# Dilated attention of the odd layer: probabilities turned 64 rows at a time inside the next unit's burst of scores, sums of values one unit later

## The chip, the cores and the metric

The kernel runs on one core of a Trainium2 chip. TensorE multiplies matrices: it loads a stationary operand (a weight load) and streams a moving operand past it into a bank of PSUM. VectorE and ScalarE do elementwise work and read those banks out, GpSimd does a few small things, and SyncE issues the DMAs. The metric is the device time of one execution in microseconds (us), the median of several runs. Before the change it is 744.56 us (three runs, 744.52 to 745.54).

## The reference, cut to what matters

The program computes a trunk of two layers over 256 tokens of width 1024, in float32: an even layer (two kinds of attention), an MLP, the odd layer, an MLP, a last norm. The change lies in the odd layer's mixer:

```python
def odd_mixer(xn, w_in, w_o, cos_f, sin_f):
    hcat = (xn @ w_in).reshape(b, s, DIL_GROUPS, 3, DIL_HEADS, HEAD_DIM)   # 3 groups, q/k/v, 16 heads, 64
    q = apply_rope(hcat[:, :, :, 0], cos_f, sin_f)
    k = apply_rope(hcat[:, :, :, 1], cos_f, sin_f)
    v = hcat[:, :, :, 2]
    return dilated_attention(q, k, v) @ w_o
# dilated_attention, of each head and each of three windows (width 128 step 1, 512 step 4, 2048 step 16):
    sc = where(valid, einsum('bqhd,bqjhd->bhqj', q, k_sel) * scale, -1e30)
    m = max(sc); e = exp(sc - m); z = sum(e); o = einsum('bhqj,bqjhd->bqhd', e / z, v_sel)
    # the three o are added with the softmax of m + log z over the windows as weights
```

Mixing three softmaxes by their denominators is one softmax over all three windows' scores, and so the kernel computes it.

## The kernel before, in words

Tokens are put in an order in which the tokens of one step-4 or step-16 window lie in blocks of 64. A query tile of 128 tokens then has 256 scores for the first window (all tokens, masked) and 64 each for the other two (its own block of 64): 384 columns. Two heads make a **unit** `u`, and there are eight units. Each is worked through in these steps:

- `qk_steps` projects q and k: 12 steps of four pairs of matmuls (L186 of 512 columns, L187 of 256), each step half of a sum over 1024 into one bank `acc`; two steps make one (block, half) pair such as (0,0). `joined` (L193 on ScalarE, L194 on VectorE) reads the finished bank out into `qk`. After a block's second bank, `rope` swaps halves with four DMAs (`sw`, L848 and L849) and turns the result on VectorE (L850, L851, L853, L856); for block 0 it also splits `q0` into a high and a low part.
- `all_values` projects v: four steps of 12 matmuls of 384 columns (L180 to L182), two steps to a bank `acc`; L818 (VectorE) and four copies L821, L822 (ScalarE) read each bank out into `v0` and `v12`.
- `scores` makes the scores of both heads for both query tiles `i`: 12 matmuls for the first window (L201, contraction over 64 rows, so head `j` sits in its own half of TensorE's rows) and 16 calls of 64x64 for the other two (L880; each float32 call is two matmuls in the trace, 32 in all). Then come mask, negated minimum, exponential, sum and scaling (L887 to L891) into the probabilities `pp`, 128x384 for each `(i, j)`.
- `turn(i, j)` transposes the probabilities of one `(i, j)`: three 128x128 transposes on TensorE (L898, with `pp` as the stationary operand) into one bank `w`, then one copy into `pts` (L900, on whichever of ScalarE and VectorE the scheduler picks).
- `mix` sums values: eight calls of 64x128 and eight of 64x64 (L913, L918; in the trace 16 and 16) into one bank `acc`, then `split` writes the high part (ScalarE, L176) and the low part (VectorE, L177) into `mixed` (`oa` for units 0 to 3, `ob` for 4 to 7).

`weave` lays the attention of unit `u-1` between the 16 projection steps of unit `u`: after the first step the scores, with `mix(u-2)` as `other()` right behind their matmuls, and later four `turn` calls a few steps apart. The weights stream in throughout: SyncE loads a raw piece, ScalarE casts it to a high part `whi` (L176) and VectorE subtracts for the low part `wlo` (L177). ScalarE and VectorE take their instructions strictly in the order in which the scheduler put them, and so does TensorE.

PSUM has two rotating sets of four banks, tagged `w` and `acc`. A new tile takes the bank of the fourth tile of its tag before it, and the first matmul into it waits until that one has been read out. The last steps, `out_steps`, project the mixed heads (L180 to L182 with `oa` or `ob`), with the last unit's attention between them.

Of the kernel before, what the change touches and what calls it, by code (L numbers as in the profile page):

```python
# [16 lines left out]
F32 = mybir.dt.float32  # L17
F32R = mybir.dt.float32r
AF = mybir.ActivationFunctionType
ALU = mybir.AluOpType  # L20
# [3 lines left out]
P = 128  # L24
D = 1024
KT = D // P
T = 256
NT = T // P
HD = 64
# [15 lines left out]
def trunk(ctx, tc, a, out):  # L45
    nc = tc.nc
# [3 lines left out]
    work = ctx.enter_context(tc.tile_pool(name="work", bufs=2))  # L50
# [26 lines left out]
    def bank(tag):  # L77
        return ps.tile([P, 512], F32, tag=tag, name=tag)
# [17 lines left out]
    ident = const.tile([P, P], F32, name="ident")  # L96
# [99 lines left out]
    def two_heads(o, qk, ts):  # L196

        for n, (a, b) in enumerate(((0, 0), (0, 1), (1, 0))):
            for j in range(2):
                pb = slice(64 * j, 64 * j + 64)  # L200
                nc.tensor.matmul(o[j], qk[pb, 0, a, ts], qk[pb, 1, b, :], start=n == 0, stop=n == 2)  # L201
# [583 lines left out]
    def odd(op, xT, s):  # L785
# [3 lines left out]
        mask = op.tile([P, NT, 384], F32, name="mask")  # L789
# [36 lines left out]
        def qk_steps(d):  # L826


            hold = {}

            def gemm(b, f, half):
                if f == 0 and half == 0:
                    hold["w"], hold["s"] = weight(), scratch([2, T], "qk")
                if half == 0:
                    hold["p"] = bank("acc")
                (wh, wl), s, pq = hold["w"], hold["s"], hold["p"]
                for k in range(4 * half, 4 * half + 4):
                    ws = slice((f * KT + k) * P, (f * KT + k + 1) * P)
                    mm2(pq, wh[:, ws], wl[:, ws], xT[:, k], k == 0, k == KT - 1)
                if half == 1:  # L840
                    joined(s[:, f], pq)
                if f == 1 and half == 1:
                    rope(b, s)

            def rope(b, s):
                sw, r1 = scratch([2, T], "sw"), scratch([2, T], "r1")
                for r in range(0, P, 64):
                    nc.sync.dma_start(sw[r:r + 32], s[r + 32:r + 64])  # L848
                    nc.sync.dma_start(sw[r + 32:r + 64], s[r:r + 32])  # L849
                nc.vector.tensor_tensor(r1, s, cosT.unsqueeze(1).broadcast_to([P, 2, T]), op=ALU.mult)  # L850
                nc.vector.tensor_tensor(sw, sw, sinT.unsqueeze(1).broadcast_to([P, 2, T]), op=ALU.mult)  # L851
                if b == 0:
                    nc.vector.tensor_tensor(r1, r1, sw, op=ALU.add)  # L853
                    split(*halves(d["q0"]), r1)
                else:
                    nc.vector.tensor_tensor(d[("q12", "k12")[b - 1]], r1, sw, op=ALU.add)  # L856
# [7 lines left out]
        turned = {}  # L864

        def attention(u, d, other, pause=2):


            probs = {}

            def scores():
                ss = {(i, j): bank("w") for i in range(NT) for j in range(2)}
                for i in range(NT):
                    two_heads([ss[i, j][:, 0:T] for j in range(2)], d["q0"], tok(i))
                for i in range(NT):
                    for g in range(2):
                        for c in range(2):
                            for j in range(2):
                                pb, own = slice(64 * j, 64 * j + 64), slice(i * P + 64 * c, i * P + 64 * c + 64)
                                nc.tensor.matmul(ss[i, j][64 * c:64 * c + 64, T + 64 * g:T + 64 * g + 64], d["q12"][pb, g, own],  # L880
                                                 d["k12"][pb, g, own], start=True, stop=True)
                other()
                for i in range(NT):
                    for j in range(2):
                        sn, pp = scratch([384], "sn"), scratch([384], "pp")
                        mn, z, rz = (work.tile([P, 1], F32, tag=v, name=v, bufs=4) for v in ("dmn", "dz", "drz"))
                        nc.vector.tensor_tensor_reduce(out=sn, in0=ss[i, j][:, 0:384], in1=mask[:, i, :], op0=ALU.add, op1=ALU.min,  # L887
                                                       scale=-(HD ** -0.5), scalar=3e38, accum_out=mn)
                        nc.scalar.activation(pp, sn, AF.Exp, bias=mn, scale=-1.0, accum_out=z)
                        nc.vector.reciprocal(rz, z)  # L890
                        nc.scalar.activation(pp, pp, AF.Copy, scale=rz)  # L891
                        probs[i, j] = pp

            def turn(i, j):
                pp = probs.pop((i, j))
                pt = bank("w")
                for b in range(3):
                    nc.tensor.transpose(pt[:, b * P:(b + 1) * P], pp[:, b * P:(b + 1) * P], ident)  # L898
                pts = turned[u, i, j] = op.tile([P, 3, P], F32, tag="pts", name="pts", bufs=6)
                nc.any.tensor_copy(out=pts, in_=pt[:, 0:384].rearrange("p (b n) -> p b n", b=3))  # L900

            wait = lambda: None
            return [scores] + [wait] * pause + [f for i in range(NT) for j in range(2) for f in (lambda i=i, j=j: turn(i, j), wait)]

        def mix(u, d, out_tag):
            pvo = bank(out_tag)
            for i in range(NT):
                pts = [turned.pop((u, i, j)) for j in range(2)]
                at = i * P
                for kk in range(NT):  # L910
                    for j in range(2):
                        cs = slice(64 * j, 64 * j + 64)
                        nc.tensor.matmul(pvo[cs, tok(i)], d["v0"][:, kk, cs], pts[j][:, kk, :], start=kk == 0, stop=False)  # L913
                for c in range(2):
                    qs = slice(64 * c, 64 * c + 64)
                    for j in range(2):
                        cs = slice(64 * j, 64 * j + 64)
                        nc.tensor.matmul(pvo[cs, at + 64 * c:at + 64 * c + 64], d["v12"][:, 2 * i + c, cs], pts[j][:, 2, qs],  # L918
                                         start=False, stop=c == 1)
            split(*halves(mixed[u // 4][:, u % 4]), pvo[:, 0:T])  # L920

        d, nd = unit_tiles(0), unit_tiles(1)
        v0, v_out = value_steps(d)
        run_all(v0)
        r = [rstd(s)]
# [17 lines left out]
        return accs, out_last(accs, mixed, wo)  # L943

    def phase(name, fn, *args):
# [108 lines left out]
```

## Time and profile before

| | |
|---|---|
| median of 3 runs | 744.56 us |
| the profiled execution | 744.4 us |
| its span on the core | 742.6 us |
| TensorE matmuls busy | 734.6 us (99%) |
| VectorE busy | 536.2 us (72%) |
| ScalarE busy | 464.2 us (63%) |
| mean granted TensorE clock | 0.999 |

The odd layer's units lie between about 304 and 550 us of the span. In the timeline a row gives the start, the length from the first start to the last end, engine, line, operation, output and inputs, tile (rows by columns of TensorE), shape, and a count. Matmuls overlap, so the cost of a matmul is the distance from its start to the next one's, not its length. In a group's row the two numbers behind the bar are the busy time in us and the mean length of one in ns.

### The profile page before, as it was taken

The numbers are of one execution on the slowest core, as the hardware profiler recorded it, in microseconds if no ns is written. First come the engines' busy times: TensorE is split into PE (matmuls) and PEld (weight loads), VectorE is DVE, ScalarE is ACT, GpSimd is POOL, SyncE is SP. The second block draws the span as 40 slices with busy tenths as digits, with TensorE's granted clock in tenths as the row PEclk, the third lists the DMA queues.
The fourth block names the chain that finished last, engine by engine and source line by source line (L and its number), as shares of the span: only waits on it lengthen the run. The fifth ranks groups of instructions, "written<-read, shape, count | busy, mean of one in ns | idle before, by whom it ended". The sixth has DMA issues, their size and how long they took to land.

```text
span 742.6 us, 12516 instructions
## 1 busy us (share of the span) xinstructions
PE 734.6 (99%) x4764; PEld 645.2 (87%) x4764; DVE 536.2 (72%) x1108; ACT 464.2 (63%) x1044; POOL 6.0 (1%) x16
## 2 busy tenths in 40 slices
PE   9999999999999999999999999999999999999996
PEld 6998998888888888989899899898998888888885
DVE  6798869666665666898777787787769665665664
ACT  6679967554554556767775866877757544554541
POOL 0100000000000000000000000000000000000000
PEclk9999999999999999999999999999999999999999
DMA  8966334555555444674655555565653545455401
GB/s 286 344 205 222 114 121 163 186 212 180 178 209 185 179 174 150 197 249 154 224 185 183 188 189 179 171 189 192 232 199 126 215 169 209 169 190 193 178 26 56
DMA packets 28107, 136.87 MB, mean 184 GB/s; under 512 B 4496, under 2 KB 7056, under 8 KB 14992
## 3 DMA queue, kind: packets, MB, share of 16 engines
q1 hardware_dynamic: 27760, 135.81, 53.4%
q8 instruction: 37, 0.61, 0.3%
q10 hardware_dynamic: 288, 0.28, 0.1%
q14 instruction: 22, 0.18, 0.1%
HBM read 127.68 MB, written 1.05 MB: 173 GB/s over the span
## 4 chain that ended last, share of the span: by engine, by line
PE 91%; ACT 3%; DMA 2%; issue 1%; DVE 1%; SPq 0%; POOLq 0%; POOL 0%; DVEq 0%; ACTq 0%
PE w L186 16%; PE acc L180 13%; PE acc L181 13%; PE acc L182 13%; PE acc L186 12%; PE w L187 8%; PE acc L187 6%; PE w L898 1%; PE acc L913 1%; PE w L201 1%; DMA raw<-in_w_v 1%; PE w L730 1%; DMA bias<-in_rpb 1%; PE w L714 1%; ACT whi L176 1%
## 5 line engine op out<-in xcount | busy, mean ns | idle before, releaser
L177 DVE TENSOR_TENSOR wlo<-raw,whi 128x512 fp32r<-128x512 f32 (+3 forms) x488 | 302.5, 664 | 63.5 <-ACT whi L176 63.0
L176 ACT CAST whi<-raw 128x512 fp32r<-128x512 f32 (+3 forms) x488 | 263.7, 602 | 82.6 <-issue 71.1
L186 PE MATMUL w<-xT,whi 128*128 128x512 f32 x512 | 179.4, 394 | 0.0
L186 PE MATMUL acc<-xT,whi 128*128 128x512 f32 x384 | 137.3, 401 | 0.0
L187 PE MATMUL w<-xT,wlo 128*128 128x256 f32 x512 | 132.8, 280 | 0.0
L186 PEld LDWEIGHTS w<-xT,whi 128*128 128x128 f32 x512 | 93.6, 187 | 18.3
L187 PEld LDWEIGHTS w<-xT,wlo 128*128 128x128 f32 x512 | 96.1, 188 | 5.5
L187 PE MATMUL acc<-xT,wlo 128*128 128x256 f32 x384 | 99.8, 280 | 0.0
L180 PE MATMUL acc<-whi,h 128*128 128x512 f32 x250 | 98.4, 393 | 0.0
L181 PE MATMUL acc<-wlo,h 128*128 128x512 f32 x250 | 97.8, 391 | 0.0
L182 PE MATMUL acc<-whi,h 128*128 128x512 f32 x250 | 97.4, 390 | 0.0
L186 PEld LDWEIGHTS acc<-xT,whi 128*128 128x128 f32 x384 | 70.0, 188 | 12.7
L193 ACT COPY up<-w 128x256 f32<-128x256 f32 x64 | 23.9, 374 | 88.4 <-PE w L186 88.4
L187 PEld LDWEIGHTS acc<-xT,wlo 128*128 128x128 f32 x384 | 72.2, 188 | 3.7
L194 DVE TENSOR_TENSOR up<-up,w 128x256 f32<-128x256 f32 x64 | 26.8, 419 | 63.0 <-ACT up L193 62.3
L180 PE MATMUL acc<-whi,xT 128*128 128x384 f32 (+2 forms) x160 | 56.6, 354 | 0.1
L181 PE MATMUL acc<-wlo,xT 128*128 128x384 f32 (+2 forms) x160 | 56.1, 351 | 0.3 <-DVE wlo L177 0.2
L182 PEld LDWEIGHTS acc<-whi,h 128*128 128x128 f32 x250 | 46.9, 188 | 10.1
L181 PEld LDWEIGHTS acc<-wlo,h 128*128 128x128 f32 x250 | 47.0, 188 | 9.8
L182 PE MATMUL acc<-whi,xT 128*128 128x384 f32 (+2 forms) x160 | 55.4, 346 | 0.0
L180 PEld LDWEIGHTS acc<-whi,h 128*128 128x128 f32 x250 | 46.9, 188 | 9.1
L181 PEld LDWEIGHTS acc<-wlo,xT 128*128 128x128 f32 x160 | 30.3, 190 | 3.0 <-DVE wlo L177 2.0
(194 smaller groups left out, 1021.3 us busy)
## 6 DMA issues: line engine op xcount, KB each, us to landing
raw<-in_w SPq DMA_DIRECT2D x64, 1024.0 KB, 4.8
raw<-in_w_oqk SPq DMA_DIRECT2D x24, 1024.0 KB, 5.1
raw<-in_w_ov SPq DMA_DIRECT2D x16, 768.0 KB, 4.5
sw<-qk SPq DMA_DIRECT2D x96, 64.0 KB, 2.2
raw<-in_w_qk SPq DMA_DIRECT2D x4, 1024.0 KB, 10.8
raw<-in_w_oe SPq DMA_DIRECT2D x4, 1024.0 KB, 7.1
raw<-in_w_oo SPq DMA_DIRECT2D x4, 1024.0 KB, 5.0
bias<-in_rpb SPq DMA_DIRECT2D x8, 256.0 KB, 5.4
```

Source lines behind the costliest of these rows:

```text
L176: a = nc.scalar.copy(hi, src).ins
L177: return a, (eng or nc.vector).tensor_tensor(lo, src, hi.bitcast(F32), op=ALU.subtract).ins
L180: nc.tensor.matmul(o, sh, mh, start=first, stop=False)
L181: nc.tensor.matmul(o, sh, ml, start=False, stop=False)
L182: nc.tensor.matmul(o, sl, mh, start=False, stop=last)
L186: both = lambda: nc.tensor.matmul(o, sh, m.rearrange("p v n -> p (v n)"), start=first, stop=last)
L187: low = lambda: nc.tensor.matmul(o[:, 0:T], sl, m[:, 0, :], start=False, stop=False)
L193: nc.scalar.copy(dst, o[:, T:2 * T])
L194: nc.vector.tensor_tensor(dst, dst, o[:, 0:T], op=ALU.add)
L201: nc.tensor.matmul(o[j], qk[pb, 0, a, ts], qk[pb, 1, b, :], start=n == 0, stop=n == 2)
L714: nc.tensor.transpose(pt[:, b * P:(b + 1) * P], pp[:, b // 2, (b % 2) * P:(b % 2 + 1) * P], ident)
L730: nc.tensor.matmul(pvo[64 * j:64 * j + 64, o], v[:, kk, h * 64:(h + 1) * 64], pts[:, 2 * j + kk, :], start=kk == 0, stop=kk == NT - 1)
```

## The change

- `turn(u, i)` now turns both heads of a query tile: 12 transposes of 64 rows by 128 columns (L899 in the changed kernel), the two row halves `r` alternating, each half into a bank of its own, so that the two run in different halves of TensorE's rows. Two copies (L902) then put them into one `pts` of both heads. Each unit has 24 such transposes in place of 12, and four copies of 384 columns as before.
- The transposes of unit `u-1` go into the burst of scores of unit `u`: query tile 0 ahead of the L201 matmuls, query tile 1 between L201 and the 64x64 scores (now L877). They use `acc` banks, not `w`.
- `mix(u-2)` (now L912 and L917) moves from behind the scores to the start of the burst of unit `u`, so a unit's values are summed one unit later than before; `v0` and `v12` get three buffers each, `pp` gets four of its own, and `pts` two that each hold both heads.
- The burst of unit `u` stands behind the second projection step of the next unit (index 1), not the first; that of unit 7 stands inside unit 7's own values (index 13), and `mix(6)`, the turns of unit 7 and `mix(7)` among `out_steps`.

```diff
-                d[n] = op.tile(shape, dt, tag=n, name=n, bufs=2)
+                d[n] = op.tile(shape, dt, tag=n, name=n, bufs=3 if n[0] == "v" else 2)
...
-            def turn(i, j):
-                pp = probs.pop((i, j))
-                pt = bank("w")
+        def turn(u, i, tag):
+
+            pt = [bank(tag) for _ in range(2)]
+            for j in range(2):
+                pp = probs.pop((u, i, j))
                 for b in range(3):
-                    nc.tensor.transpose(pt[:, b * P:(b + 1) * P], pp[:, b * P:(b + 1) * P], ident)
-                pts = turned[u, i, j] = op.tile([P, 3, P], F32, tag="pts", name="pts", bufs=6)
-                nc.any.tensor_copy(out=pts, in_=pt[:, 0:384].rearrange("p (b n) -> p b n", b=3))
-
-            wait = lambda: None
-            return [scores] + [wait] * pause + [f for i in range(NT) for j in range(2) for f in (lambda i=i, j=j: turn(i, j), wait)]
+                    at = slice((3 * j + b) * 64, (3 * j + b) * 64 + 64)
+                    for r in range(2):
+                        rows = slice(64 * r, 64 * r + 64)
+                        nc.tensor.transpose(pt[r][:, at], pp[rows, b * P:(b + 1) * P], ident[rows, rows])
+            pts = turned[u, i] = op.tile([P, 6, P], F32, tag="pts", name="pts", bufs=2)
+            for r in range(2):
+                nc.any.tensor_copy(out=pts[:, :, 64 * r:64 * r + 64], in_=pt[r][:, 0:384].rearrange("p (b n) -> p b n", b=6))
...
-        weave(qk_steps(nd) + all_values(nd), attention(0, d, lambda: None, 3), 3)
-        for u in range(2, 8):
-            pd, d, nd = d, nd, unit_tiles(u)
-            side = attention(u - 1, d, lambda: mix(u - 2, pd, "acc"))
-
-            weave(qk_steps(nd) + all_values(nd), side + [lambda: mix(6, d, "acc")] if u == 7 else side)
+        def burst(u):
+
+            def step():
+                if u > 1:
+                    mix(u - 2, units[u - 2], "acc")
+                if u > 0:
+                    turn(u - 1, 0, "acc")
+                scores(u, units[u], lambda: turn(u - 1, 1, "acc") if u > 0 else None)
+            return step
+
+        for u in range(1, 8):
+            units.append(unit_tiles(u))
+            placed = {3 if u == 1 else 1: burst(u - 1)}
+            if u == 7:
+                placed[13] = burst(7)
+            beside(qk_steps(units[u]) + all_values(units[u]), placed)
         accs, wo = open_accs(), {}
-        side = attention(7, nd, lambda: None) + [lambda: mix(7, nd, "w")]
-        weave([f for k in range(6) for f in out_steps(accs, mixed, wo, k)], side)
+
+        def last_turn():
+            mix(6, units[6], "w")
+            for i in range(NT):
+                turn(7, i, "w")
+
+        beside([f for k in range(6) for f in out_steps(accs, mixed, wo, k)], {6: last_turn, 9: lambda: mix(7, units[7], "w")})
```

`beside(main, placed)` runs the main steps in order and a placed step behind the one of its index. In `scores(u, d, between)` the call `between()` stands between the two kinds of scores.

**TensorE, a burst in the middle of the layer.** A row gives a line, an operation, its output and inputs (numbered tensors are a unit's own) and the shape; `x12` counts repeats, and a bracket names the engine whose progress the first of them waits for. Before:

```order
L186 MATMUL acc<-xT,whi 128x512
L187 MATMUL acc<-xT,wlo 128x256
L201 MATMUL w<-q_4212 128x256 x6
L201 MATMUL w<-q_4212 128x256 [waits PE_49]
L201 MATMUL w<-q_4212 128x256 [waits Activation_49]
L201 MATMUL w<-q_4212 128x256 x4
L880 MATMUL w<-k_4214,q_4213 64x64 [waits DVE_49]
L880 MATMUL w<-k_4214,q_4213 64x64 x15
L913 MATMUL acc<-pts,v_3833 64x128 x4
L918 MATMUL acc<-pts,v_3834 64x64 x4
L913 MATMUL acc<-pts,v_3833 64x128 x4
L918 MATMUL acc<-pts,v_3834 64x64 x4
```

Now, at the same place:

```order
L912 MATMUL acc<-pts,v_3809 64x128 [waits PE_49]
L912 MATMUL acc<-pts,v_3809 64x128 x3
L917 MATMUL acc<-pts,v_3810 64x64 x4
L912 MATMUL acc<-pts,v_3809 64x128 x4
L917 MATMUL acc<-pts,v_3810 64x64 x4
L899 MATMUL acc<-ident,pp 128x64 [waits DVE_49,Activation_49] x2
L899 MATMUL acc<-ident,pp 128x64 x10
L201 MATMUL w<-q_4571 128x256 x12
L899 MATMUL acc<-ident,pp 128x64 [waits DVE_49] x2
L899 MATMUL acc<-ident,pp 128x64 x10
L877 MATMUL w<-k_4573,q_4572 64x64 x16
L186 MATMUL acc<-xT,whi 128x512 [waits Activation_49]
```

The values now come first, then the first turn, the L201 scores, the second turn and the 64x64 scores. The two first transposes of the second turn, one to each of its banks, wait for VectorE.

**VectorE, at the same place.** `sn` is the masked score, `qk` the projection's sum, `oa` the mixed heads, `v` the values. Before:

```order
L818 TENSOR_SCALAR v_4215<-acc,rstd 128x128
L177 TENSOR_TENSOR wlo<-raw,whi 128x512 x5
L887 ISA sn,dmn<-w,mask 128x384
L887 ISA dmn 128x1
L887 ISA sn,dmn<-w,mask 128x384
L887 ISA dmn 128x1
L887 ISA sn,dmn<-w,mask 128x384
L887 ISA dmn 128x1
L890 RECIPROCAL drz<-dz 128x1 x2
L177 TENSOR_TENSOR oa<-acc,oa 128x256
```

Now:

```order
L818 TENSOR_SCALAR v_4574<-acc,rstd 128x128
L856 TENSOR_TENSOR k_4573<-r_4871,sw 128x512
L177 TENSOR_TENSOR wlo<-raw,whi 128x512 x3
L194 TENSOR_TENSOR qk<-qk,acc 128x256
L177 TENSOR_TENSOR wlo<-raw,whi 128x512 x2
L177 TENSOR_TENSOR oa<-acc,oa 128x256
L177 TENSOR_TENSOR wlo<-raw,whi 128x512
L902 COPY pts<-acc 128x6x64
L883 ISA sn,dmn<-w,mask 128x384
L883 ISA dmn 128x1
```

The sum of bank (0,0) (L194) and the low part of the mixed heads (`oa`) now stand ahead of the masked scores, with two pieces of weights between them.

**ScalarE, at the same place.** Before:

```order
L176 CAST whi<-raw 128x512 x6
L821 ACTIVATE v_4598<-acc,rstd 64x128
L822 ACTIVATE v_4598<-acc,rstd 64x128
L821 ACTIVATE v_4598<-acc,rstd 64x128
L822 ACTIVATE v_4598<-acc,rstd 64x128
L176 CAST whi<-raw 128x512 x2
L889 ACTIVATE pp,dz<-sn,dmn 128x384 x2
L176 CAST oa<-acc 128x256
```

Now:

```order
L176 CAST whi<-raw 128x512 x6
L821 ACTIVATE v_4575<-acc,rstd 64x128
L822 ACTIVATE v_4575<-acc,rstd 64x128
L821 ACTIVATE v_4575<-acc,rstd 64x128
L822 ACTIVATE v_4575<-acc,rstd 64x128
L176 CAST whi<-raw 128x512
L193 COPY qk<-acc 128x256
L176 CAST whi<-raw 128x512
L176 CAST oa<-acc 128x256
L902 COPY pts<-acc 128x6x64 x3
```

The copies of the second value bank, a cast, the copy of bank (0,0) and another cast stand ahead of the high part of the mixed heads.

More of the change, by code (lines that the diff above doesn't have):

```diff
@@ new lines, in turn @@
+        def turn(u, i, tag):
+            pt = [bank(tag) for _ in range(2)]
+            for j in range(2):
+                pp = probs.pop((u, i, j))
+                for b in range(3):
+                    at = slice((3 * j + b) * 64, (3 * j + b) * 64 + 64)
[5 more added lines that the diff above has]
+                nc.any.tensor_copy(out=pts[:, :, 64 * r:64 * r + 64], in_=pt[r][:, 0:384].rearrange("p (b n) -> p b n", b=6))
@@ L907, in mix @@
             for i in range(NT):
-                pts = [turned.pop((u, i, j)) for j in range(2)]
+                pts = turned.pop((u, i))
                 at = i * P
@@ L912, in mix @@
                         cs = slice(64 * j, 64 * j + 64)
-                        nc.tensor.matmul(pvo[cs, tok(i)], d["v0"][:, kk, cs], pts[j][:, kk, :], start=kk == 0, stop=False)
+                        nc.tensor.matmul(pvo[cs, tok(i)], d["v0"][:, kk, cs], pts[:, 3 * j + kk, :], start=kk == 0, stop=False)
                 for c in range(2):
@@ L917, in mix @@
                         cs = slice(64 * j, 64 * j + 64)
-                        nc.tensor.matmul(pvo[cs, at + 64 * c:at + 64 * c + 64], d["v12"][:, 2 * i + c, cs], pts[j][:, 2, qs],
+                        nc.tensor.matmul(pvo[cs, at + 64 * c:at + 64 * c + 64], d["v12"][:, 2 * i + c, cs], pts[:, 3 * j + 2, qs],
                                          start=False, stop=c == 1)
             split(*halves(mixed[u // 4][:, u % 4]), pvo[:, 0:T])
-        d, nd = unit_tiles(0), unit_tiles(1)
+        units = [unit_tiles(0)]
+        d = units[0]
         v0, v_out = value_steps(d)
```

52 lines of the change are left out of this document (27 added, 25 removed).

## The prediction

> **What bounds the kernel now.** I read the page first, then the waits of TensorE, then its timeline through one unit of the odd layer, and last the timelines of ScalarE and VectorE there.
>
> ```profile
> span 742.6 us, 12516 instructions
> PE 734.6 (99%) x4764; PEld 645.2 (87%) x4764; DVE 536.2 (72%) x1108; ACT 464.2 (63%) x1044; POOL 6.0 (1%) x16
> ...
> PE w L880 <- DVE k L856: 0.2, 1, 0.2
> ```
>
> TensorE (PE) is busy for 99% of the span, and past the program's start the longest wait for another engine in its list is 0.2 us. So time is saved by taking slots off TensorE, and any new wait of TensorE costs its full length. A whole burst of scores, and one turn:
>
> ```profile
> 408.92 0.28 PE L187 MATMUL acc<-xT,wlo 128*128 128x256 f32 x1
> 409.13 0.98 PE L201 MATMUL w<-q 64*128 64x256 f32 x12
> 410.04 0.69 PE L880 MATMUL w<-k,q 64*64 64x64 f32 x32
> 410.67 0.66 PE L913 MATMUL acc<-pts,v 128*64 128x128 f32 x8
> ...
> 411.82 0.40 PE L918 MATMUL acc<-pts,v 128*64 128x64 f32 x8
> 412.15 0.50 PE L186 MATMUL acc<-xT,whi 128*128 128x512 f32 x1
> 412.49 0.28 PE L187 MATMUL acc<-xT,wlo 128*128 128x256 f32 x1
> ...
> 417.41 0.28 PE L187 MATMUL acc<-xT,wlo 128*128 128x256 f32 x1
> 417.53 0.39 PE L186 MATMUL acc<-xT,whi 128*128 128x512 f32 x1
> 417.76 0.28 PE L187 MATMUL acc<-xT,wlo 128*128 128x256 f32 x1
> 417.88 0.49 PE L898 MATMUL w<-ident,pp 128*128 128x128 f32 x3
> 418.13 0.48 PE L186 MATMUL acc<-xT,whi 128*128 128x512 f32 x1
> 418.44 0.28 PE L187 MATMUL acc<-xT,wlo 128*128 128x256 f32 x1
> ```
>
> Undisturbed, L187 to L187 takes 0.35 us (417.41 to 417.76): 0.12 for 256 columns and 0.23 for 512. The burst stretches that distance to 3.57 (408.92 to 412.49), so it costs 3.22: 0.09 on entering (0.21 less the slot of 0.12), L201 0.91, L880 0.63, the values 1.48, and 0.11 on leaving (0.34 less 0.23). A turn stretches it to 0.68 and costs 0.33, or 0.11 for each transpose; four turns make 1.32. Attention thus costs a unit 4.54 us of TensorE.
>
> **What a 64-row transpose costs.** No such transpose is in the trace; these groups bound it:
>
> ```profile
> L898 PE MATMUL w<-ident,pp 128*128 128x128 f32 x96 | 15.7, 272 | 0.1
> L880 PE MATMUL w<-k,q 64*64 64x64 f32 x256 | 5.6, 224 | 0.2 <-DVE k L856 0.2
> L898 PEld LDWEIGHTS w<-ident,pp 128*128 128x128 f32 x96 | 12.0, 140 | 1.8 <-ACT pp L891 0.3
> L201 PEld LDWEIGHTS w<-q 64*128 64x128 f32 x96 | 6.2, 185 | 1.9 <-issue 1.8
> L880 PEld LDWEIGHTS w<-k,q 64*64 64x64 f32 x256 | 4.5, 134 | 1.5 <-DVE k L856 0.5
> ```
>
> Streaming 64 columns of float32 in place of 128 shortens a matmul by about 50 ns (272 to 224). The load of a transpose (140) is nearly as short as that of 64 columns (134) and not like L201's 128 (185). L880 shows how fast tiles follow one another in separate parts of the array: 32 matmuls in groups of four, 0.63 us for eight groups, at most 0.08 each with entry and drain. L201 shows two heads side by side in the two row halves: 12 matmuls in 0.91 us is six pairs, where twelve slots of 0.12 would be 1.44. So a pair of 64-row transposes, the work of one old transpose, costs 0.055 to 0.08 if its load stays short, and 0.11, as now, if it doesn't. I take 0.06.
>
> The Trainium skill speaks against this: "TensorE: Matmul & The Clock Gate", section "LDWEIGHTS (loading the stationary operand)", gives a load P/1.2 ns by its P columns, whatever the rows. By it, as an estimate, a pair would cost at least 107 ns and nothing would be gained. The trace agrees for L201's loads and not for L898's, which are 45 ns shorter at equal columns; no row shows a half-height transpose.
>
> **The new burst without waits**, by the order on TensorE: entering 0.09, values 1.48, first turn 0.47 (six pairs of 0.06, 0.06 for the first load and 0.05 for L201's), L201 0.72 (six slots of 0.12, its entry and drain now in the turns), second turn 0.44 (six pairs and a drain of 0.08), 64x64 scores 0.63, leaving 0.11. That is 3.94 against 4.54: 0.60 saved. Five bursts (units 2 to 6) look so: 3.0 us.
>
> The ends, in the same prices: before, the values of units 6 and 7 stand alone, and so do unit 7's scores. For the values:
>
> ```profile
> 524.49 0.34 PE L182 MATMUL acc<-whi,xT 128*128 128x384 f32 x1
> 524.75 0.66 PE L913 MATMUL acc<-pts,v 128*64 128x128 f32 x8
> ...
> 526.24 0.44 PE L180 MATMUL acc<-whi,xT 128*128 128x384 f32 x1
> 526.52 0.34 PE L181 MATMUL acc<-wlo,xT 128*128 128x384 f32 x1
> ```
>
> That is 2.03 less two slots of 0.17: 1.68. Unit 0's scores are the same on both sides. From there, before: six bursts 19.3, two lone values 3.4, unit 7's scores 1.7 (0.09 + 0.91 + 0.63 + 0.11), 32 turns 10.6: 35.0. After: unit 1 without values 2.5, five bursts 19.7, unit 7 with its 64x64 scores ten rows later 3.3 + 0.8, values 6 with both last turns 2.5, values 7 1.7: 30.5. **Without waits the change saves 4.5 us.**
>
> **The wait that it adds.** `turn` now takes `acc` banks, four in rotation. Counted in the order of the code: projection (0,0), values, first turn (two), second turn (two). So the second turn's banks are those of projection (0,0) and of the values, and both must have been read out by then. Behind the waiting transposes stand the 64x64 scores and all projections. By the sums above the second turn is due 2.76 us after the burst starts (0.09 + 1.48 + 0.47 + 0.72). The values' bank is free when VectorE has written the low part of `oa`, and VectorE gets there only after L194 of (0,0) and two pieces of weights, and L194 only after ScalarE has finished the copies of the second value bank (L822), a cast and L193. When does L822 end, counted from the start of projection (0,0)?
>
> ```profile
> 351.39 0.36 ACT L822 ACTIVATE v<-acc,rstd 64x128 f32<-64x128 f32 x1
> 379.86 0.36 ACT L822 ACTIVATE v<-acc,rstd 64x128 f32<-64x128 f32 x1
> 411.16 0.36 ACT L822 ACTIVATE v<-acc,rstd 64x128 f32<-64x128 f32 x1
> 440.71 0.36 ACT L822 ACTIVATE v<-acc,rstd 64x128 f32<-64x128 f32 x1
> 470.46 0.36 ACT L822 ACTIVATE v<-acc,rstd 64x128 f32<-64x128 f32 x1
> 499.55 0.36 ACT L822 ACTIVATE v<-acc,rstd 64x128 f32<-64x128 f32 x1
> ...
> 348.05 0.40 PE L186 MATMUL acc<-xT,whi 128*128 128x512 f32 x1
> 377.84 0.40 PE L186 MATMUL acc<-xT,whi 128*128 128x512 f32 x1
> 407.64 0.40 PE L186 MATMUL acc<-xT,whi 128*128 128x512 f32 x1
> ```
>
> Projection (0,0) starts every 29.79 us (348.05, 377.84, 407.64), and L822 ends 3.7, 2.4, 3.9, 3.6, 3.6 and 2.9 us behind it. What follows has these lengths:
>
> ```profile
> 406.78 3.23 ACT L176 CAST whi<-raw 128x512 fp32r<-128x512 f32 x6
> ...
> 409.72 1.89 DVE L177 TENSOR_TENSOR wlo<-raw,whi 128x512 fp32r<-128x512 f32 x3
> ...
> L193 ACT COPY qk<-acc 128x256 f32<-128x256 f32 x48 | 17.2, 370 | 23.7 <-PE acc L186 23.7
> L194 DVE TENSOR_TENSOR qk<-qk,acc 128x256 f32<-128x256 f32 x48 | 19.5, 416 | 8.3 <-ACT qk L193 8.0
> L177 DVE TENSOR_TENSOR oa<-acc,oa 128x256 fp32r<-128x256 f32 x4 | 1.7, 425 | 0.7 <-ACT oa L176 0.7
> ```
>
> A cast 0.54 (3.23/6), L193 0.37, L194 0.35 to where VectorE can go on, two pieces 1.2 (1.89/3 each), the low part 0.43: 2.9. The bank is free 2.9 us after L822's end. It is due 5.57 after the start of (0,0): 2.81 for its eight pairs of 0.35, and 2.76. The wait is L822's lag less 2.67: 1.0, 0, 1.2, 0.9, 0.9, 0.2 by the six units, mean 0.7. I take 0.9, since the lag should grow: the masked scores now start behind a longer burst, and the copies, swaps and pieces queued behind them slip with them. A lower bound is 0.2 (the quickest pass of ScalarE's queue, six casts and four copies behind the first value step), an upper one 1.4. Five bursts: 4.5 us. At the ends the same banks cost about 2.2: unit 1 (the second turn comes sooner, 1.28 after the start, and needs only (0,0)) about 0.8, unit 7 about 0.8, the last turn behind `mix(6)` about 0.6 (L176 0.37, L177 0.43 and the way to ScalarE, less 0.4 for the first turn).
>
> The Trainium skill's "TensorEngine Tiling (Array Packing)", "PSUM Bottleneck", warns of just this, that faster tiles leave the reading of PSUM as the bound.
>
> **The sum:** -4.5 + 4.5 + 2.2 = +2.2 us on the profiled 744.4, or 746.7 on the median of 744.56.
>
> **What costs nothing.** The copies into `pts` keep number and width; each is wanted a unit later. SP issues unit 1's first value load four `sw` DMAs later, and weights are loaded four tiles ahead. A unit's probabilities are wanted 29 us after their scores. If a masked score came so late that it held a `w` bank, the next burst would show it; it has a unit's time.
>
> **The rivals.** (1) The gain stands and the waits are short: the fast lag of 2.4 becomes the rule, since ScalarE no longer waits for turns between the projections. With 0.2 a burst and 1.2 at the ends: -4.5 + 1.0 + 1.2 = -2.3, 742.3; with no wait at all 740.1. Against it: five of six lags are 2.9 or more. (2) Waits of half the size, 0.5 a burst and 1.9 at the ends: -0.1, 744.4. (3) The half-height load is as long as L201's, and a pair costs 0.11: 96 pairs give back 0.05 each, 4.8, while a later second turn shortens each of eight waits by 0.3, 2.4: 2.2 + 2.4 = +4.6, 749.2. That the two halves don't overlap at all would be slower still; L201's pairs speak against it.
>
> **How the numbers follow.** Forecast 0.42 (745.2 to 748.2 by waits of 0.6 to 1.2), rival 1 0.25, rival 2 0.18, rival 3 0.15. The limit of what can be told from no change is 0.2%, 1.5 us: 743.1 and 746.05. Slower: 0.30 of the forecast's share and rival 3's 0.15, 0.45. Same: 0.12 of the forecast's and 0.15 of rival 2, 0.27. Faster: 0.28. The range runs from rival 1 with waits near nothing to rival 3: 741.6 to 749.4.
>
> **What would show it.** In the changed trace: 24 L899 in two groups per burst, about 0.4 us each from first to last start (right) or 0.65 (rival 3); TensorE idle before the second group, released by VectorE's `oa` L177, near 0.9 us in most bursts; the distance of the bursts about 30.1 us (29.79 - 0.60 + 0.9). I am wrong if the list of TensorE's waits has no such row, or if the second turn's wait ends on something else.

## The result and the profile after

| | before | after |
|---|---|---|
| median, 6 runs each, same chip | 744.79 us (744.52 to 745.54) | 749.42 us (748.67 to 750.07) |
| ratio | | 1.006, 95% interval 1.005 to 1.007 |
| the profiled execution, and its span | 744.4, 742.6 us | 750.07, 748.3 us |

The change makes the kernel 4.6 us slower. The forecast was +2.2 us (746.7). The measured median lies at the upper end of the stated range of 741.6 to 749.4, and above the 745.2 to 748.2 that the forecast itself was given.

The page after the change (busy us, share of the span, instructions of each engine):

```profile
span 748.3 us, 12683 instructions
PE 733.3 (98%) x4860; PEld 642.4 (86%) x4860; DVE 538.7 (72%) x1113; ACT 462.6 (62%) x1039; POOL 6.1 (1%) x16
```

TensorE's waits after the change (what waited, for which engine's tile and line; us in total, times, longest):

```profile
PE acc L899 <- DVE oa L177: 3.0, 4, 0.7
PE acc L899 <- ACT pts L902: 1.2, 1, 1.2
...
PE acc L899 <- DVE ob L177: 0.8, 1, 0.8
```

TensorE is busy 1.3 us less (734.6 before) in a span that is 5.7 us longer. Before, its list held nothing above 0.2 us behind the start; now the transposes L899 wait five times for the low part of the mixed heads (`oa` L177 four times, `ob` L177 once), and once for a copy into `pts`. Here is one burst on TensorE, from the last projection ahead of it to the first pair behind:

```profile
410.19 0.40 PE L186 MATMUL acc<-xT,whi 128*128 128x512 f32 x1
410.51 0.66 PE L912 MATMUL acc<-pts,v 128*64 128x128 f32 x8
...
412.00 0.59 PE L899 MATMUL acc<-ident,pp 64*128 64x64 f32 x12
412.40 0.96 PE L201 MATMUL w<-q 64*128 64x256 f32 x12
413.20 0.21 PE L899 MATMUL acc<-ident,pp 64*128 64x64 f32 x1
414.16 0.58 PE L899 MATMUL acc<-ident,pp 64*128 64x64 f32 x11 [0.74 <-DVE oa L177]
414.67 0.69 PE L877 MATMUL w<-k,q 64*64 64x64 f32 x32
...
415.64 0.28 PE L187 MATMUL acc<-xT,wlo 128*128 128x256 f32 x1
```

The first turn takes 0.40 us (412.00 to 412.40) for six pairs, so 0.07 a pair with the way in. The second is let in with one transpose at 413.20, and the next comes at 414.16: it takes 1.47 us in all. From L186 to L187 the burst stretches 5.45 us (410.19 to 415.64) where the two projection slots of 0.23 would take 0.46 or 0.47: it costs 4.98, of which about 1.0 is the wait.

The same stretch on ScalarE and on VectorE shows what the second turn waits for:

```profile
410.71 0.36 ACT L822 ACTIVATE v<-acc,rstd 64x128 f32<-64x128 f32 x1
411.10 0.62 ACT L176 CAST whi<-raw 128x512 fp32r<-128x512 f32 x1
411.74 0.37 ACT L193 COPY qk<-acc 128x256 f32<-128x256 f32 x1
412.01 0.62 ACT L176 CAST whi<-raw 128x512 fp32r<-128x512 f32 x1
412.53 0.38 ACT L176 CAST oa<-acc 128x256 fp32r<-128x256 f32 x1
...
412.48 1.28 DVE L177 TENSOR_TENSOR wlo<-raw,whi 128x512 fp32r<-128x512 f32 x2
413.69 0.42 DVE L177 TENSOR_TENSOR oa<-acc,oa 128x256 fp32r<-128x256 f32 x1
```

The low part ends at 414.11 (413.69 + 0.42) and the transposes go on at 414.16. Bursts 2 to 6 all look like this: their first L912 stand at 380.19, 410.51, 440.85, 471.18 and 501.51, 30.33 us apart, where the distance before was 29.79.

**Where the 4.6 us lie.** From the first L201 of the odd layer to the layer's last projection of mixed heads, TensorE took 231.4 us before and 235.9 after: 4.55 more. The profiled execution after the change had also lost 1.15 us ahead of that point, where nothing was changed. Over the nine profiled executions of this case that point lies between 325.0 and 326.7 us, so this is the spread of runs. In the layer, measured between the first value steps of the units, the start (to unit 1's first value step) gained 0.94, the next stretch 0.56, the five bursts lost 0.54 each (2.7), and the end from unit 7's values on lost 3.34.

### The profile page after: what moved, and what is told of

Read it like the earlier page. It is cut to its first block, busy times and chain, and to the rows that moved or that the text cites. A ratio compares the mean times of both kernels' runs of the same rounds, so it can differ in the third digit from the quotient of the medians.

```text
span 748.3 us, 12683 instructions
## 1 busy us (share of the span) xinstructions
PE 733.3 (98%) x4860; PEld 642.4 (86%) x4860; DVE 538.7 (72%) x1113; ACT 462.6 (62%) x1039; POOL 6.1 (1%) x16
## 4 chain that ended last, share of the span: by engine, by line
PE 86%; ACT 7%; DVE 3%; issue 1%; DMA 1%; SPq 0%; POOLq 0%; POOL 0%; DVEq 0%
PE w L186 16%; PE acc L180 13%; PE acc L181 13%; PE acc L182 13%; PE acc L186 10%; PE w L187 8%; PE acc L187 5%; ACT whi L176 3%; DMA raw<-in_w_c 1%; DVE wlo L177 1%; PE w L714 1%; PE w L730 1%; ACT v L822 1%; ACT v L821 1%; PE w L877 1%
## 5 line engine op out<-in xcount | busy, mean ns | idle before, releaser
L177 DVE TENSOR_TENSOR wlo<-raw,whi 128x512 fp32r<-128x512 f32 (+3 forms) x488 | 303.6, 665 | 72.7 <-ACT whi L176 71.7
L186 PE MATMUL w<-xT,whi 128*128 128x512 f32 x512 | 179.4, 394 | 0.0
L186 PE MATMUL acc<-xT,whi 128*128 128x512 f32 x384 | 134.6, 396 | 0.0
L187 PE MATMUL w<-xT,wlo 128*128 128x256 f32 x512 | 132.8, 280 | 0.0
L186 PEld LDWEIGHTS w<-xT,whi 128*128 128x128 f32 x512 | 93.6, 187 | 18.3
L187 PEld LDWEIGHTS w<-xT,wlo 128*128 128x128 f32 x512 | 96.1, 188 | 5.5
L187 PE MATMUL acc<-xT,wlo 128*128 128x256 f32 x384 | 99.8, 280 | 0.0
L181 PE MATMUL acc<-wlo,h 128*128 128x512 f32 x250 | 97.8, 391 | 0.0
L186 PEld LDWEIGHTS acc<-xT,whi 128*128 128x128 f32 x384 | 69.8, 187 | 13.6
L193 ACT COPY up<-w 128x256 f32<-128x256 f32 x64 | 23.9, 374 | 88.6 <-PE w L186 88.6
L187 PEld LDWEIGHTS acc<-xT,wlo 128*128 128x128 f32 x384 | 72.0, 188 | 3.8
L194 DVE TENSOR_TENSOR up<-up,w 128x256 f32<-128x256 f32 x64 | 26.9, 420 | 62.9 <-ACT up L193 62.0
L181 PE MATMUL acc<-wlo,xT 128*128 128x384 f32 (+2 forms) x160 | 56.1, 351 | 0.6 <-DVE wlo L177 0.6
L181 PEld LDWEIGHTS acc<-wlo,h 128*128 128x128 f32 x250 | 47.0, 188 | 9.8
L193 ACT COPY qk<-acc 128x256 f32<-128x256 f32 x48 | 17.7, 368 | 30.8 <-PE acc L186 30.6
```

Source lines behind the costliest of these rows:

```text
L177: return a, (eng or nc.vector).tensor_tensor(lo, src, hi.bitcast(F32), op=ALU.subtract).ins
L181: nc.tensor.matmul(o, sh, ml, start=False, stop=False)
L186: both = lambda: nc.tensor.matmul(o, sh, m.rearrange("p v n -> p (v n)"), start=first, stop=last)
L187: low = lambda: nc.tensor.matmul(o[:, 0:T], sl, m[:, 0, :], start=False, stop=False)
L193: nc.scalar.copy(dst, o[:, T:2 * T])
L194: nc.vector.tensor_tensor(dst, dst, o[:, 0:T], op=ALU.add)
```

## The experiments

Each is compared with the kernel before on the same chip; for the first four that is 744.88 us, for the last three 744.93. "After" below is the changed kernel.

### 1. Take away what makes the second turn wait

The weight pieces of the next tile are held back until the mixed heads' two parts and the copies into `pts` have been issued, on ScalarE and VectorE alike; the copies into `pts` get fixed engines (three on ScalarE, one on VectorE).

```diff
-        prefetch(j + LOAD_AHEAD, j + SPLIT_AHEAD)
+        behind = state.pop("behind", ())
+        with ExitStack() as held:
+            for ins in behind:
+                held.enter_context(tc.issue_after(ins))
+            prefetch(j + LOAD_AHEAD, j + SPLIT_AHEAD)
...
-                nc.any.tensor_copy(out=pts[:, :, 64 * r:64 * r + 64], ...)
+                copy = nc.vector.tensor_copy if i and r else nc.scalar.copy
+                done = copy(pts[:, :, 64 * r:64 * r + 64], ...).ins
+                state["behind"] = state.get("behind", ()) + (done,)
...
-                    mix(u - 2, units[u - 2], "acc")
+                    state["behind"] = mix(u - 2, units[u - 2], "acc")
```

> The changed kernel with one thing moved: the weight pieces that ScalarE and VectorE had ahead of the mixed heads' split are held behind that split and behind the copies of the turned probabilities (which get fixed engines, as the scheduler had them: three on ScalarE, one on VectorE). TensorE's order stays as it is. Theory (the second turn waits for the values' bank because two weight pieces and the late copy of projection (0,0) stand ahead of it): the wait of about 1.0 us per burst in the changed kernel falls to 0.2 or less, the distance of bursts from 30.33 to about 29.4 us, the time from 749.4 to 743.5 to 745. Rival (the wait belongs to the bank rotation, whatever stands in the queues, or it moves to the next projection's bank): the distance stays at 30 us or more, the time above 748.

Measured: 742.84 us (742.44 to 743.94), ratio 0.9971 (0.996 to 0.9983), a little below the 743.5 to 745 that the theory gave. The timeline of a burst on TensorE, and the low part on VectorE (lines are shifted by four: L903 is L899, L205 is L201, L881 is L877, L190 is L186, L181 is L177):

```profile
408.26 0.40 PE L190 MATMUL acc<-xT,whi 128*128 128x512 f32 x1
...
410.08 0.58 PE L903 MATMUL acc<-ident,pp 64*128 64x64 f32 x12
410.47 0.96 PE L205 MATMUL w<-q 64*128 64x256 f32 x12
411.28 0.53 PE L903 MATMUL acc<-ident,pp 64*128 64x64 f32 x12
411.74 0.69 PE L881 MATMUL w<-k,q 64*64 64x64 f32 x32
...
412.70 0.28 PE L191 MATMUL acc<-xT,wlo 128*128 128x256 f32 x1
...
410.60 0.42 DVE L181 TENSOR_TENSOR oa<-acc,oa 128x256 fp32r<-128x256 f32 x1 [1.07 <-ACT oa L180]
```

The low part ends at 411.02, ahead of the second turn, which now takes 0.46 us. The burst costs 3.97 (408.26 to 412.70, less 0.47); the prediction's price without waits was 3.94. The bursts stand 29.33 apart. So the changed kernel's loss of 4.6 us, and a gain of 2 us that it hid, hang on the order on two engines that are 62% and 72% busy.

### 2. The same order with whole-height transposes

```diff
-                    at = slice((3 * j + b) * 64, (3 * j + b) * 64 + 64)
-                    for r in range(2):
-                        rows = slice(64 * r, 64 * r + 64)
-                        nc.tensor.transpose(pt[r][:, at], pp[rows, b * P:(b + 1) * P], ident[rows, rows])
+                    nc.tensor.transpose(pt[j][:, b * P:(b + 1) * P], pp[:, b * P:(b + 1) * P], ident)
```

> The changed kernel with 128x128 transposes in place of those of 64 rows, one bank for each head; places, banks and order otherwise as in the change. Theory (a 64-row pair costs 0.06 us where a whole transpose costs 0.11, and the wait swallows what that saves): each turn 0.7 to 0.8 us long in place of 0.4, with two more changes of tile shape, but the second turn's wait falls from about 1.0 to 0.1 to 0.4, so that the distance of bursts stays within 0.3 us of 30.33 and the time at 749 to 751.5. Rival (the two row halves don't run side by side, so the halving saves nothing): turns as long as now, the time unchanged or lower by the waits, 745 to 748.

Measured: 748.91 us (748.77 to 749.31), ratio 1.005 (1.0034 to 1.0067), just below the 749 to 751.5 that were expected. The two turns of a burst (L896):

```profile
411.35 0.87 PE L896 MATMUL acc<-ident,pp 128*128 128x128 f32 x6
412.15 0.97 PE L201 MATMUL w<-q 64*128 64x256 f32 x12
413.05 0.88 PE L896 MATMUL acc<-ident,pp 128*128 128x128 f32 x6
413.85 0.69 PE L877 MATMUL w<-k,q 64*64 64x64 f32 x32
```

Each turn takes 0.80 us, L201 0.90 in place of 0.80, and the second turn comes late enough that it waits for nothing: the list of waits has no row for `oa`, only one of 0.5 us for a copy into `pts`. The bursts stand 30.17 apart. So the short transposes are worth 0.84 us a burst (the distance of 30.17 less 29.33 of experiment 1), which is just what the three pieces add up to: 0.80 + 0.90 + 0.80 against 0.40 + 0.80 + 0.46. The two kernels lie 6.1 us apart (748.91 less 742.84), but they also differ in the order of the weight pieces and in the waits outside these bursts, so 6.1 is not the price of the transposes alone. In the changed kernel the wait takes the whole gain back: 749.42 with half heights, 748.91 with whole ones.

### 3. Half heights alone

The kernel before with each transpose split into two of 64 rows into two `w` banks; where they stand and when values are summed stays as before.

```diff
-                pt = bank("w")
+                pt = [bank("w") for _ in range(2)]
...
-                    nc.tensor.transpose(pt[:, b * P:(b + 1) * P], pp[:, b * P:(b + 1) * P], ident)
+                    for r in range(2):
+                        rows = slice(64 * r, 64 * r + 64)
+                        nc.tensor.transpose(pt[r][:, b * 64:b * 64 + 64], pp[rows, b * P:(b + 1) * P], ident[rows, rows])
```

> The kernel before with the 64-row transposes alone: each of the 32 turns stays where it was, between projections, as six transposes of 64 rows into two w banks with a copy from each. Theory (a pair costs 0.06, but entering and leaving the half-height tile shape costs 0.09 + 0.06 and 0.08 + 0.11): a turn costs about 0.5 us in place of 0.33, 32 x 0.17 = 5.5 us more, 749 to 751. Rival (a change of tile shape costs nothing of its own): a turn costs 0.2, 740 to 741.

Measured: 751.30 us (751.11 to 751.47), ratio 1.0082 (1.0067 to 1.0097), 0.3 above the theory's range. One turn among the projections:

```profile
390.09 0.28 PE L187 MATMUL acc<-xT,wlo 128*128 128x256 f32 x1
390.30 0.40 PE L900 MATMUL w<-ident,pp 64*128 64x64 f32 x6
390.63 0.50 PE L186 MATMUL acc<-xT,whi 128*128 128x512 f32 x1
390.97 0.28 PE L187 MATMUL acc<-xT,wlo 128*128 128x256 f32 x1
```

L187 to L187 takes 0.88 us, so a turn costs 0.53 (less 0.35 for the pair), where the whole-height turn cost 0.33. Entering adds 0.09 (0.21 less the slot of 0.12), three pairs take 0.33, leaving adds 0.11. Thirty-two turns at 0.20 more make 6.4 us, and the kernel is 6.4 us slower. In the changed kernel's burst there are twelve in a row, and none of their neighbours is a tile of 128x128. Ahead of L201, whose tile shape (64 rows by 128) is theirs too, they take 0.40 us, behind it 0.46 (experiment 1), and between the values and the 64x64 scores, neither of their shape, 0.52 (experiment 4); six whole-height ones take 0.80 in the burst (experiment 2). So the move into the burst is not a detail of the change: where the turns stood before, the short transposes lose. No run has twelve in a row among projections, so how much of the loss is due to the short run and how much to the neighbours is not shown.

### 4. Leave the weights as they are and move the values away

Here `mix` stands between L201 and the second turn, so its bank is no longer the one that the second turn takes; `pts` gets a third buffer.

```diff
-                if u > 1:
-                    mix(u - 2, units[u - 2], "acc")
                 if u > 0:
                     turn(u - 1, 0, "acc")
-                scores(u, units[u], lambda: turn(u - 1, 1, "acc") if u > 0 else None)
+                scores(u, units[u], between)   # between: mix(u - 2, ...), then turn(u - 1, 1, "acc")
```

> The changed kernel with the values moved from the start of the burst to between the L201 scores and the second turn, so that the second turn's banks are those of projection (0,0) and of the first turn, and three pts buffers. Theory (which bank is due when decides the wait): the second turn comes 3.0 us after the start, its banks are free at about 2.1 and 2.8 us, so its wait falls to 0.2 or less; one more change of tile shape costs 0.1 to 0.2; the distance of bursts 29.4 to 29.6 and the time 744.5 to 746. Rival (VectorE is late by a fixed amount and any second turn waits for it): the wait stays near 1 us and the time at 749 or above.

Measured: 745.45 us (744.74 to 746.09, 10 runs), ratio 1.0005 (0.9995 to 1.0014). The burst has one more change of tile shape, and in four bursts of five no wait at the second turn:

```profile
411.52 0.59 PE L899 MATMUL acc<-ident,pp 64*128 64x64 f32 x12
412.04 0.69 PE L877 MATMUL w<-k,q 64*64 64x64 f32 x32
...
411.18 1.89 DVE L177 TENSOR_TENSOR wlo<-raw,whi 128x512 fp32r<-128x512 f32 x3
412.98 0.42 DVE L177 TENSOR_TENSOR oa<-acc,oa 128x256 fp32r<-128x256 f32 x1
```

The second turn takes 0.52 us and the bursts stand 29.47 apart. One is 29.88: there the second turn takes 0.93, since ScalarE's queue is 0.66 us later against projection (0,0) and the copy of the first turn, whose bank the second one takes, comes late with it. Of the 4.6 us lost, 4.0 come back, though nothing holds the weight pieces: three of them still stand ahead of the low part of the mixed heads, which ends at 413.40, almost 2 us behind the start of the second turn. TensorE doesn't wait for it, because the values' bank is no longer the one that is due. That the wait was for the values' bank is shown by this and the first experiment from two sides. Unit 1's wait of 1.2 us for a copy into `pts`, which this edit doesn't touch, stands in its list of waits as before.

### 5. Hold the weights back on VectorE alone

As experiment 1, but the pieces wait only for the low part of the mixed heads, on VectorE; ScalarE's order is that of the changed kernel.

```diff
-                    mix(u - 2, units[u - 2], "acc")
+                    state["behind"] = mix(u - 2, units[u - 2], "acc")[1:]   # the low part alone
```

> The changed kernel with the next tile's low weight pieces held only on VectorE, behind the low part of the mixed heads; ScalarE's order is as in the changed kernel. Theory (the wait is mostly VectorE's two pieces of 0.6 us that stand between L194 and the low part): the low part then ends about 1.2 us earlier, the second turn's wait falls from 1.0 to at most 0.3 us, the bursts stand 29.4 to 29.7 us apart, and the whole takes 743.5 to 746 us. Rival (ScalarE's late copies L822 and casts decide, and VectorE's pieces only fill the time until they arrive): the wait stays at 0.7 us or more, the bursts stay 30.0 us or more apart, 747.5 to 749.5 us.

Measured: 748.43 us (747.89 to 749.37), ratio 1.0049 (1.0034 to 1.0064): the rival's time, and not the theory's. The bursts are not alike, and neither forecast fits all of them: they stand 29.91, 30.88, 30.08, 29.60 and 29.58 apart. The second of them on the three engines (lines shifted by three):

```profile
406.34 0.40 PE L189 MATMUL acc<-xT,whi 128*128 128x512 f32 x1
...
413.46 0.59 PE L902 MATMUL acc<-ident,pp 64*128 64x64 f32 x11 [0.53 <-DVE oa L180]
...
406.39 3.22 ACT L179 CAST whi<-raw 128x512 fp32r<-128x512 f32 x6
...
412.57 0.38 ACT L179 CAST oa<-acc 128x256 fp32r<-128x256 f32 x1
...
412.98 0.42 DVE L180 TENSOR_TENSOR oa<-acc,oa 128x256 fp32r<-128x256 f32 x1 [0.37 <-ACT oa L179]
```

VectorE now runs the low part as soon as ScalarE's high part is there (412.95), so its two pieces no longer delay it. But ScalarE is late itself: its six casts begin at 406.39, with projection (0,0) of 406.34, and in the changed kernel they begin 1.2 us ahead of it (406.35 against 407.58, rows below). In this burst, the worst of the five, the first turn waits for ScalarE too: it takes 0.73 us in place of 0.40, held by the copies L825 of the second value bank. In the two last bursts, where ScalarE kept its old place, the low part ended 5.78 us after the start of (0,0) in place of 6.53, and the wait fell to about 0.3 us as expected (a second turn of 0.73 less 0.46); in the other three ScalarE's queue had slipped by 0.3 to 1.3 us and the second turn waited 0.6 to 0.85.

```profile
407.58 0.40 PE L186 MATMUL acc<-xT,whi 128*128 128x512 f32 x1
...
406.35 3.23 ACT L176 CAST whi<-raw 128x512 fp32r<-128x512 f32 x6
```

So VectorE's two pieces are worth 0.75 us of the wait where nothing else moves. What is left there, about 0.3, went in experiment 1, where ScalarE's casts were held as well and no burst waited; no run held ScalarE alone. What made ScalarE slip in three bursts of this kernel isn't settled: its copies of the first value bank wait there for VectorE's L821, which is itself late by 1.3 us against TensorE, and no run followed that further back.

### 6. The ends

Experiment 1's kernel, with `mix(6)` two output steps earlier and the last turns and `mix(7)` one later; experiment 1's kernel ran beside it again.

```diff
-            mix(6, units[6], "w")
-        beside(..., {6: last_turn, 9: lambda: mix(7, units[7], "w")})
+        beside(..., {4: lambda: mix(6, units[6], "w"), 7: last_turn, 10: lambda: mix(7, units[7], "w")})
```

> The first experiment's kernel (weight pieces held on both engines), with unit 6's values two steps earlier among the output steps and both last turns and unit 7's values one step later, so that the reading of unit 6's values has about 3 steps of cover before the last turns need their banks. If the waits that are left at the end come from too little distance between values and turns: the last turns run in 0.9 to 1.0 us without a wait, one more change of tile shape costs about 0.2, and it takes 0.3 to 0.7 us less than the first experiment's kernel on the same chip, 742.2 to 742.6 us. If what is left at the end is a wait for ScalarE's late casts of weights and mixed heads, the wait moves to the next output step and the time is the same within 0.2 us.

> The first experiment's kernel once more, beside the other two on the same chip: 742.4 to 743.2 us.

Measured: 742.42 us (741.89 to 743.12), ratio 0.9964 (0.9951 to 0.9976), beside 742.72 (742.10 to 743.39), ratio 0.9973 (0.9961 to 0.9985). The last turns, first as in experiment 1, then here:

```profile
538.68 0.77 PE L903 MATMUL w<-ident,pp 64*128 64x64 f32 x15
539.68 0.59 PE L903 MATMUL w<-ident,pp 64*128 64x64 f32 x9 [0.23 <-DVE ob L181]
540.20 0.39 PE L184 MATMUL acc<-oa,whi 128*128 128x256 f32 x1
```

```profile
541.12 0.96 PE L903 MATMUL w<-ident,pp 64*128 64x64 f32 x24
542.01 0.39 PE L184 MATMUL acc<-ob,whi 128*128 128x256 f32 x1
```

They took 1.52 us and take 0.89. From unit 7's first value step to the layer's last projection the trace is 0.45 us shorter (41.00 against 41.45), the 0.63 less what the added change of shape costs; the times differ by 0.3 us, and their intervals overlap, so in the time this gain is not shown. Both kernels beat the one before and the changed one.

## Why the prediction was right or wrong

Set against its own sum, in us, for the odd layer. The measured column comes from the profiled execution after the change, with the times without waits from experiments 1 and 6. The ends' part without waits is what is left of the 4.55 when the other rows are taken off:

| term | predicted | measured |
|---|---|---|
| five bursts without waits | -3.0 (3.94 for 4.54) | -2.85 (3.97) |
| projections and values between them | 0 | +0.5 (0.1 a unit) |
| second turn's wait in five bursts | +4.5 (0.9 each) | +5.05 (1.0 each) |
| the ends without waits | -1.5 | about -1.15 |
| the ends' waits | +2.2 | about +3.0 |
| sum | +2.2 | +4.55 |

**The price of a pair was right.** It was taken as 0.06 us between bounds of 0.055 and 0.11. Twelve transposes take 0.40 us in the first turn and 0.46 undisturbed in the second, 0.07 to 0.08 a pair with the way in and out. Rival 3, the long load, falls by this row of the changed kernel's groups (mean length in ns behind the bar), where each load is as short as the whole-height one of 140:

```profile
L899 PEld LDWEIGHTS acc<-ident,pp 64*128 64x128 f32 x168 | 7.1, 138 | 6.9 <-DVE oa L177 3.7 <-ACT pts L902 1.3 <-DVE ob L177 0.9
```

A whole-height transpose took 0.11 us before, and 0.13 in experiment 2 (0.80 for six): a pair is cheaper. Within a turn the matmuls start in twos, less than 0.01 us apart, and the twos follow one another every 0.06 us: the two halves do run side by side. The rule of the Trainium skill that spoke against the change ("TensorE: Matmul & The Clock Gate", section "LDWEIGHTS (loading the stationary operand)") made it at least 107 ns a pair, as an estimate from its columns; the first turn's 0.40 us for six is at most 67, so the trace does not agree. Nor do the loads that the prediction called in agreement have the 107 ns that it gives for 128 columns: L201's took 185.

**The wait was right in kind and place, and its size in part by luck.** Every link named stands in the trace: L822, cast, L193, cast and high part on ScalarE, L194, two pieces and low part on VectorE, then the transposes. The rule "lag less 2.67" with L822's lag after the change, 3.5 us in every burst (411.07 less 407.58), gives 0.8; measured is 1.0, chiefly since the low part came 3.04 us behind L822 instead of 2.9. What had been a lag between 2.4 and 3.9 became a steady one. The 0.9 was chosen because the lag should grow, but its mean went only from 3.35 to 3.5, so it is luck that the choice came out near. The steady lag undid rival 1, in which the short lag would become the rule; that happens only when the pieces are held on both engines (lag 2.46 in experiment 1, and its 742.84 is close to rival 1's 742.3).

The Trainium skill's "TensorEngine Tiling (Array Packing)", "PSUM Bottleneck", had warned that the reading of PSUM may be the next bound. Here the trace agrees in part: TensorE does wait 1.0 us a burst for a bank to be read out, but the two read-outs take only about 0.4 us each, and the wait goes when the weight pieces ahead of them are held (experiment 1).

**The ends' waits were mis-sized, by 0.8.** Unit 1's was put at 0.8, "needs only (0,0)". It is 1.4, and it ends on another bank:

```profile
352.13 0.21 PE L899 MATMUL acc<-ident,pp 64*128 64x64 f32 x1
353.50 0.58 PE L899 MATMUL acc<-ident,pp 64*128 64x64 f32 x11 [1.15 <-ACT pts L902]
...
351.00 1.15 ACT L176 CAST whi<-raw 128x512 fp32r<-128x512 f32 x2
...
352.96 0.87 ACT L902 COPY pts<-acc 128x384 f32<-128x384 f32 x2
...
351.66 1.29 DVE L177 TENSOR_TENSOR wlo<-raw,whi 128x512 fp32r<-128x512 f32 x2 [0.89 <-ACT whi L176]
352.87 0.41 DVE L194 TENSOR_TENSOR qk<-qk,acc 128x256 f32<-128x256 f32 x1
```

L194 is done with (0,0) at 353.28; the transposes start at 353.50, just behind the first copy into `pts` (one such copy takes 0.48, from 352.96). In the program as built, unit 1's second turn is given a bank of its own first turn, three tiles back, and not that of (0,0), the fourth; in experiment 1's program it is given that of (0,0). So the rule that a tile takes the bank of the fourth one before it, on which the prediction counted, doesn't hold at every place, and how the scheduler chose isn't settled. But the other bank explains only 0.2 of the 0.6 that were missed: with (0,0) alone the wait would have been about 1.2 (353.28 less 352.13). The rest is that L194 itself was late, behind two casts on ScalarE and two pieces on VectorE. With the weight pieces held (experiment 1) this turn takes 0.46. The last turns' wait was put at 0.6 and is 0.63 (1.52 against 0.89). Unit 7's second turn was put at 0.8 and lost about 0.3. And one wait was not foreseen, an output step that needs the bank of unit 7's last values, which ScalarE copies late:

```profile
536.72 0.28 PE L182 MATMUL acc<-oa,wlo 128*128 128x256 f32 x1
537.46 0.38 PE L180 MATMUL acc<-oa,whi 128*128 128x256 f32 x1 [0.47 <-ACT v L822]
```

The start-to-start distance is 0.74 where 0.12 is usual, so 0.62.

**The gain without waits was over-counted, by about 1.0.** Bursts cost 3.97 and not 3.94 (0.15 in five). Between the bursts a unit's projections and values take 25.36 us with or without waits, against 25.25 before (29.79 less 4.54): 0.1 a unit, which no term of the sum held. It shows in the value steps, whose 384-column matmuls follow one another every 176.6 ns in place of 174.7 (48 a unit, 0.09). They are as slow in experiment 2, whose transposes are whole, and not in experiment 3 (174.7), so it comes with the new order and not with the transposes; why isn't settled. The other 0.35 lies at the ends.

So the wait of the second turn decided the sign, as forecast, and the size missed by 1.0 of gain and 1.4 of waits (0.55 in the bursts, 0.8 at the ends). Both errors were on the optimistic side, which put the result at the top of the range. That this top lay just there is luck: it was set by rival 3, whose 749.2 is nearly the measured time for a reason that did not occur.

## What to carry to other kernels

When a faster piece of work is to write into rotating banks, count whose banks they are at every place where it stands (first and last rounds apart), check the count against the program, and follow the reading of each back through both reading engines: it was not the copies that were slow here, but prefetched weights that the scheduler put in front of them, on engines with a third of their time free. Holding the prefetch behind the read-out on both engines (experiment 1) turned +4.6 into -2.0 us; holding it on VectorE alone (experiment 5) gave back only about 1 us. Transposes of half height paid here in runs of twelve inside the burst, where no neighbour is a tile of 128x128, and lost in runs of six among projections.

## What the runs showed of the hardware that was not expected

- A short run of half-height transposes loses to whole-height ones: six cost 0.53 us among projections of 128x128 tiles and three whole ones 0.33 (experiment 3); twelve in the burst take 0.40 to 0.52, by their neighbours, and six whole ones there 0.80 (experiment 2).
- L201 itself became cheaper between turns of its own shape, 0.80 us in place of 0.90 between whole-height turns; the prediction had 0.72.
- The wait did not vary. Before the change L822's lag went from 2.4 to 3.9 us with the unit; after it, it is 3.49 or 3.50 in all five, and the distances of the bursts are equal to 0.02 us. It is not the wait that holds the engines in step: in experiment 2 the bursts have no wait, and the lag is 3.48 or 3.49 in all five as well. What does isn't settled.
